# Two matmuls of one pair change places in the first entry of each group

## The chip, the cores and the metric

The kernel runs on one core of one Trainium2 chip. The metric is the device time of one execution in microseconds; lower is better. The engines are named as the profile names them: PE is TensorE's matmuls and PEld its weight loads, DVE is VectorE, ACT ScalarE, POOL GpSimd, SP SyncE.

## The reference, cut to what matters

One hybrid decoder block on 256 tokens of width 2048, all in float32:

```
x = layer_norm(ALPHA*x + 0.5*swiglu(x, ffn1 gate, up, down))     # D_FF 5632
mix = hybrid_mixer(x)        # x @ w_in, then attention heads and a gated linear recurrence, then @ w_out
x = layer_norm(ALPHA*x + mix)
x = layer_norm(ALPHA*x + 0.5*swiglu(x, ffn2 gate, up, down))
x = x + sigmoid(x @ w_ple_gate) * (p @ w_ple_proj)
```

`swiglu(x, g, u, d)` is `(silu(x @ g) * (x @ u)) @ d`. Nearly all arithmetic is matrix products of 256 tokens with weights that are read once from memory.

## The kernel before, in words

**Precision by parts.** TensorE multiplies in a reduced float32 format (fp32r). Each operand is therefore held as two: hi, the value cast to the format, and lo, the rest. A product takes hi*hi, hi*lo and lo*hi. For weights ScalarE makes hi (line 104) and VectorE lo (line 110).

**Entries.** The weights come in a planned order as entries of 256 rows x 512 columns, two halves (k = 0, 1) of 128 rows side by side. `load` starts an entry's DMA on SP's queue, `prepare_hi` and `prepare_lo` split it, `take` hands it to the matmuls, `done` gives its slot back. There are 7 slots for split entries and 10 buffers for raw ones. Both halves of an entry are split by one instruction each, but for the very first entry, which is split half by half. The order of the instructions on every engine is the order in which the program writes them.

**Groups.** Two kinds of matmul exist. `group_b` and the down products keep the activations stationary and stream 512 weight columns (`mm_moving_w`, three matmuls of 512 columns each). `group_a` keeps the weights stationary: a group computes 512 output columns as four blocks (b = 0 to 3) of 128, one PSUM bank each, over 8 entries (j = 0 to 7). For each entry `tokens_a` runs over the blocks and, inside, over the two halves. Per block and half stands a pair, `mm_stationary_w`: first a matmul with weights hi that streams the tokens' hi and lo, 2 x 256 = 512 columns, into the whole bank; then one with weights lo that streams the tokens' hi alone, 256 columns, into the bank's first half. The two half banks are added at the end by `evac_a` (ScalarE copies one, VectorE adds the other). An entry has 8 pairs, a group 64.

**Where `group_a` is used.** In each of the two feed-forward parts 11 chunks have a gate group and an up group. From the fifth group on, after every second entry (in the last chunk every entry), `product` runs part of a down projection on activations that are ready: 12 matmuls of 512 columns, put together in a scheme of seven products for four blocks. The first gate group of the second part is a boundary group: it goes over its 8 entries twice, with 128 tokens each, so that the normalisation before it can end meanwhile. In the mixer `channels` calls `group_a` six times (three for the recurrence's input, three for its gate). After each entry `tick` lets waiting work go a step: pieces of the recurrence and of attention, some of which put plain float32 matmuls and transposes on TensorE.

**Start flags.** The first matmul of a bank in a group (entry 0, half 0) clears the bank; all others add to it.

The change touches `mm_stationary_w`, `tokens_a`, `group_a` and `channels`.

Of the kernel before, what the change touches and what calls it, by code (L numbers as in the profile page):

```python
# [15 lines left out]
KB = D // P  # L16
# [24 lines left out]
class Block:  # L41
# [220 lines left out]
    def mm(self, out, lhsT, rhs, start, stop):  # L262
        self.nc.tensor.matmul(out, lhsT=lhsT, rhs=rhs, start=start, stop=stop, skip_group_check=True)  # L263

    def mm_stationary_w(self, bank, b, hi, lo, k, kb, tok, start, stop):
        bv = bank.rearrange("p (s t) -> p s t", s=2)
        c = slice(b * P, (b + 1) * P)
        self.mm(bv[:, :, tok], hi[:, k, c], self.xT[:, kb, :, tok], start, False)
        self.mm(bv[:, 0, tok], lo[:, k, c], self.xT[:, kb, 0, tok], False, stop)

    def mm_moving_w(self, bank, act, hi, lo, start, stop):
        ah, al = act
# [5 lines left out]
        ts = slice(t * P, (t + 1) * P)  # L278
        return self.xT[:, kb, 0, ts], self.xT[:, kb, 1, ts]

    def tokens_a(self, e, j, banks, tok, first, on_block=None):
        for b in range(4):
            for k in range(2):
                kb = 2 * j + k
                self.mm_stationary_w(banks[b], b, e["hi"], e["lo"], k, kb, tok, kb == 0 and first, kb == KB - 1)
            if on_block and j == 7:
                on_block(b, banks[b])

# [2 lines left out]
            kb = 2 * j + k  # L291
            self.mm_moving_w(bank[:, cols], self.x_act(kb, t), e["hi"][:, k, cols], e["lo"][:, k, cols], kb == 0, kb == KB - 1)

    def group_a(self, on_block, boundary=False, step=2):
        banks = [self.bank() for _ in range(4)]
        if not boundary:
            for j in range(8):
                e = self.take()
                self.tokens_a(e, j, banks, slice(0, 256), True, on_block)
                self.done(e)  # L300
                self.tick()
                if j % step == step - 1:
                    self.product()
            return
        es = []
        self.limit = self.taken + 8
        for j in range(8):
            es.append(self.take())
            self.tokens_a(es[j], j, banks, slice(0, P), True)
            if j == 1:  # L310
                self.advance_lo(self.ready)
            if j in HOOKS:
                self.ln_transpose(1, HOOKS.index(j))
        self.limit = len(self.plan)
        self.res_q.append(self.ln_residual())
        for j in range(8):
            self.tokens_a(es[j], j, banks, slice(P, 256), False, on_block)
            self.done(es[j])
            self.tick()
# [447 lines left out]
    def channels(self):  # L767
        got = []

        def on_block(b, bank):  # L770
            if b == 0:
                got.append(self.wide())
            self.evac_a(bank, got[0][:, b, :])

        self.group_a(on_block)
        return got[0]

    def mixer(self):
# [156 lines left out]
```

## Time and profile before

| | |
|---|---|
| median of three runs | 1920.38 us (1919.65 to 1920.59) |
| profiled execution | 1922.0 us, its span 1919.9 us |
| mean granted TensorE clock | 0.996 |
| busy: PE, PEld, DVE, ACT, POOL | 98%, 84%, 79%, 57%, 13% |
| read from memory | 413.38 MB, 216 GB/s over the span |
| matmuls with stationary weights, hi and lo | 3216 and 3216 |

The span is the time from the first to the last instruction of the profiled execution. Busy times are unions of recorded instructions; a matmul is recorded until its modelled end, and the next one starts before that, so the distance from one start to the next says what a matmul takes of TensorE's time. The chain that ended last is followed back from the last instruction, at each step to what released it.

### The profile page before, as it was taken

The numbers are of one execution on the slowest core, as the hardware profiler recorded it, in microseconds if no ns is written. First come the engines' busy times: TensorE is split into PE (matmuls) and PEld (weight loads), VectorE is DVE, ScalarE is ACT, GpSimd is POOL, SyncE is SP. The second block draws the span as 40 slices with busy tenths as digits, with TensorE's granted clock in tenths as the row PEclk, the third lists the DMA queues.
The fourth block names the chain that finished last, engine by engine and source line by source line (L and its number), as shares of the span: only waits on it lengthen the run. The fifth ranks groups of instructions, "written<-read, shape, count | busy, mean of one in ns | idle before, by whom it ended". The sixth has DMA issues, their size and how long they took to land.

```text
span 1919.9 us, 26885 instructions
## 1 busy us (share of the span) xinstructions
PE 1878.9 (98%) x10004; PEld 1614.0 (84%) x10004; DVE 1522.9 (79%) x1889; ACT 1090.7 (57%) x1440; POOL 242.4 (13%) x173
## 2 busy tenths in 40 slices
PE   8999999999999999999999999999999999999899
PEld 7888888888888777887888898888888888887787
DVE  6698887887888879577676966888879888888774
ACT  6565555555655556566655454655556555556552
POOL 0010000000010116001010250000000100011160
PEclk9999999999999999999999999999999999999999
DMA  9678688788786876655455656787887868878572
GB/s 355 218 192 265 209 254 234 207 262 244 221 253 190 232 239 211 195 178 163 143 184 178 208 181 182 241 221 216 255 253 201 260 207 253 246 207 252 179 231 76
DMA packets 216770, 417.23 MB, mean 217 GB/s; under 512 B 13232, under 2 KB 15936, under 8 KB 216640
## 3 DMA queue, kind: packets, MB, share of 16 engines
q1 hardware_dynamic: 193856, 370.42, 58.1%
q0 software_dynamic: 22784, 45.10, 13.8%
q8 instruction: 78, 1.28, 0.3%
q14 instruction: 52, 0.43, 0.1%
HBM read 413.38 MB, written 2.10 MB: 216 GB/s over the span
## 4 chain that ended last, share of the span: by engine, by line
PE 87%; DVE 7%; issue 2%; ACT 2%; DMA 1%; POOL 1%; SPq 0%; ACTq 0%; DVEq 0%; POOLq 0%
PE mm L263 86%; DVE lo L110 3%; DVE raw L82 1%; DVE w L370 1%; ACT hi L104 1%; DMA raw<-in_w_in_dram 0%; DMA raw<-in_ffn_w_gate_dram 0%; PE mm L505 0%; DVE w L556 0%; ACT w L64 0%; POOL w L110 0%; DVE w L65 0%; DMA raw<-in_ffn_w_down_dram 0%; DVE acc L495 0%; DVE acc L428 0%
## 5 line engine op out<-in xcount | busy, mean ns | idle before, releaser
L104 ACT CAST hi<-raw 128x1024 fp32r<-128x1024 f32 (+1 forms) x786 | 809.6, 1049 | 545.3 <-PE mm L263 470.6
L263 PE MATMUL mm<-xT,hi 128*128 128x512 f32 (+1 forms) x3216 | 1104.8, 390 | 6.2 <-DVE xT L65 5.2
L110 DVE TENSOR_TENSOR lo<-raw,hi 128x1024 fp32r<-128x1024 f32 (+1 forms) x786 | 950.3, 1250 | 100.1 <-ACT hi L104 90.4
L263 PE MATMUL mm<-xT,lo 128*128 128x256 f32 (+1 forms) x3216 | 888.7, 276 | 0.0
L263 PEld LDWEIGHTS mm<-xT,hi 128*128 128x128 f32 x3216 | 605.2, 188 | 132.2 <-ACT hi L104 6.5
L263 PEld LDWEIGHTS mm<-xT,lo 128*128 128x128 f32 x3216 | 606.6, 189 | 6.2 <-DVE lo L110 0.7
L263 PE MATMUL mm<-hi,w 128*128 128x512 f32 x1464 | 483.2, 394 | 13.3 <-DVE acc L428 11.0
L263 PEld LDWEIGHTS mm<-hi,w 128*128 128x128 f32 x1464 | 276.5, 189 | 76.2 <-ACT hi L104 13.7
L263 PE MATMUL mm<-lo,w 128*128 128x512 f32 x732 | 288.0, 394 | 0.0
L85 POOL DMA_DIRECT2D raw<-in_ffn_w_down_dram x80 | 96.0, 1218 | 1116.4 <-DVE raw L82 546.8
L263 PE MATMUL mm<-hi,xT 128*128 128x512 f32 (+1 forms) x544 | 168.8, 386 | 0.0
L428 DVE TENSOR_TENSOR acc<-acc,mm 128x512 f32<-128x512 f32 x124 | 84.9, 684 | 100.8 <-PE mm L263 100.8
L263 PEld LDWEIGHTS mm<-lo,w 128*128 128x128 f32 x732 | 138.5, 189 | 23.4
L263 PEld LDWEIGHTS mm<-hi,xT 128*128 128x128 f32 x544 | 101.3, 189 | 19.3
L263 PE MATMUL mm<-lo,xT 128*128 128x512 f32 (+1 forms) x272 | 104.0, 382 | 3.6 <-DVE lo L110 3.6
L370 DVE TENSOR_TENSOR w<-mm,w 128x256 f32<-128x256 f32 x200 | 83.6, 419 | 28.1 <-ACT w L369 27.6
L82 DVE TENSOR_TENSOR raw<-raw,raw 128x1024 f32<-128x1024 f32 x80 | 97.8, 1222 | 1.4
L369 ACT COPY w<-mm 128x256 f32<-128x256 f32 x200 | 72.6, 365 | 25.9 <-PE mm L263 22.3
L541 ACT ACTIVATE w<-w 128x256 f32<-128x256 f32 x88 | 36.8, 418 | 67.3 <-DVE w L370 67.3
L64 ACT CAST w<-qk 128x512 fp32r<-128x512 f32 (+1 forms) x42 | 25.5, 609 | 83.6 <-DVE qk L455 40.4
L542 DVE TENSOR_TENSOR w<-w,w 128x256 f32<-128x256 f32 x88 | 38.0, 432 | 43.4 <-ACT w L541 43.4
L508 ACT ACTIVATE qk<-mm,par 128x128 f32<-128x128 f32 x96 | 36.1, 456 | 54.3 <-PE mm L505 54.1
(136 smaller groups left out, 872.6 us busy)
## 6 DMA issues: line engine op xcount, KB each, us to landing
raw<-in_ffn_w_up_dram SPq DMA_DIRECT2D x176, 512.0 KB, 5.0
raw<-in_ffn_w_down_dram SPq DMA_DIRECT2D x176, 512.0 KB, 5.3
raw<-in_ffn_w_gate_dram SPq DMA_DIRECT2D x175, 512.0 KB, 5.5
raw<-in_w_in_dram SPq DMA_DIRECT2D x88, 512.0 KB, 4.5
raw<-in_ffn_w_down_dram POOLq DMA_DIRECT2D x80, 512.0 KB, 7.4
raw<-in_w_out_dram SPq DMA_DIRECT2D x32, 512.0 KB, 4.6
raw<-in_w_ple_gate_dram SPq DMA_DIRECT2D x32, 512.0 KB, 6.1
w<-in_ln_g_dram SPq DMA_DIRECT2D x12, 256.0 KB, 6.3
```

Source lines behind the costliest of these rows:

```text
L64: self.nc.scalar.copy(hi, src)
L82: self.nc.vector.tensor_tensor(a, a, b, op=ALU.add)
L85: self.nc.gpsimd.dma_start(a, src, accum_op=ALU.add)
L104: self.nc.scalar.copy(e["hi"][:, k, :], e["raw"][:, k, :])
L110: eng.tensor_tensor(e["lo"][:, k, :], e["raw"][:, k, :], e["hi"][:, k, :].bitcast(F32), op=ALU.subtract)
L263: self.nc.tensor.matmul(out, lhsT=lhsT, rhs=rhs, start=start, stop=stop, skip_group_check=True)
L369: self.nc.scalar.copy(c, bank[:, 256:])
L370: self.nc.vector.tensor_tensor(dst, bank[:, :256], c, op=ALU.add)
L428: self.nc.vector.tensor_tensor(a, a, bank, op=op)
L508: nc.scalar.activation(z[:, q, :], bank[:, q * P:(q + 1) * P], AF.Identity, bias=self.par[:, p0 + 16 + kb:p0 + 17 + kb], scale=self.par[:, ...
L541: nc.scalar.activation(s, g, AF.Sigmoid)
L542: nc.vector.tensor_tensor(g, g, s, op=ALU.mult)
```

## The change

In the pair of block 0, half 1, the matmul with weights lo is issued before the one with weights hi. In the feed-forward parts this is done in the first entry of each group (j = 0), in the mixer's `channels` groups in all eight entries. The number of instructions, their operands and the data moved stay the same; the two flags follow the place in the pair.

```
-    def mm_stationary_w(self, bank, b, hi, lo, k, kb, tok, start, stop):
+    def mm_stationary_w(self, bank, b, hi, lo, k, kb, tok, start, stop, low_first=False):
         bv = bank.rearrange("p (s t) -> p s t", s=2)
         c = slice(b * P, (b + 1) * P)
-        self.mm(bv[:, :, tok], hi[:, k, c], self.xT[:, kb, :, tok], start, False)
-        self.mm(bv[:, 0, tok], lo[:, k, c], self.xT[:, kb, 0, tok], False, stop)
+        high = bv[:, :, tok], hi[:, k, c], self.xT[:, kb, :, tok]
+        low = bv[:, 0, tok], lo[:, k, c], self.xT[:, kb, 0, tok]
+        one, two = (low, high) if low_first else (high, low)
+        self.mm(*one, start, False)
+        self.mm(*two, False, stop)
...
-    def tokens_a(self, e, j, banks, tok, first, on_block=None):
+    def tokens_a(self, e, j, banks, tok, first, on_block=None, turn=False):
...
-                self.mm_stationary_w(banks[b], b, e["hi"], e["lo"], k, kb, tok, kb == 0 and first, kb == KB - 1)
+                self.mm_stationary_w(banks[b], b, e["hi"], e["lo"], k, kb, tok, kb == 0 and first, kb == KB - 1,
+                                     b == 0 and k == 1 and (turn or j == 0))
...
-    def group_a(self, on_block, boundary=False, step=2):
+    def group_a(self, on_block, boundary=False, step=2, turn=False):
...
-                self.tokens_a(e, j, banks, slice(0, 256), True, on_block)
+                self.tokens_a(e, j, banks, slice(0, 256), True, on_block, turn)
...
-        self.group_a(on_block)
+        self.group_a(on_block, turn=True)
```

The last two lines are those of `channels`.

## Rows read from the trace of the kernel before

**Rows 1.** Page: slices (PEclk in tenths) and the chain, by engine.

```profile
PEclk9999999999999999999999999999999999999999
...
PE 87%; DVE 7%; issue 2%; ACT 2%; DMA 1%; POOL 1%; SPq 0%; ACTq 0%; DVEq 0%; POOLq 0%
```

**Rows 2.** Timeline of PE at 982 us; columns: start us, duration us, instruction, tiles.

```profile
982.00 0.39 PE L263 MATMUL mm<-xT,hi 128*128 128x512 f32 x1
982.22 0.28 PE L263 MATMUL mm<-xT,lo 128*128 128x256 f32 x1
982.34 0.39 PE L263 MATMUL mm<-xT,hi 128*128 128x512 f32 x1
```

**Rows 3.** Timeline of PE at 1134 us.

```profile
1134.00 0.40 PE L263 MATMUL mm<-xT,hi 128*128 128x512 f32 x1
1134.23 0.28 PE L263 MATMUL mm<-xT,lo 128*128 128x256 f32 x1
1134.35 0.39 PE L263 MATMUL mm<-xT,hi 128*128 128x512 f32 x1
```

**Rows 4.** Groups by line and shape, 12.84 to 104.4 us; busy us, mean ns, idle.

```profile
L263 PE MATMUL mm<-xT,hi 128*128 128x512 f32 x263 | 92.4, 395 | 0.0
L263 PE MATMUL mm<-xT,lo 128*128 128x256 f32 x262 | 73.7, 281 | 0.0
```

**Rows 5.** Groups by line and shape, 180 to 480 us.

```profile
L263 PE MATMUL mm<-xT,hi 128*128 128x512 f32 x616 | 211.6, 389 | 0.0
L263 PE MATMUL mm<-xT,lo 128*128 128x256 f32 x615 | 169.9, 276 | 0.0
```

**Rows 6.** Windows: length, busy us (x count) by engine, PEclk, DMA share, GB/s.

```profile
795.10:821.60 26.50, 26.50 (x151) 23.29 (x150) 10.86 (x12) 18.85 (x30) 2.40 (x1) 1.00 0.50 152
934.50:958.60 24.10, 22.65 (x137) 19.97 (x136) 13.64 (x24) 17.64 (x29) 3.09 (x2) 1.00 0.45 128
1124.40:1199.70 75.30, 75.30 (x428) 66.13 (x427) 49.05 (x64) 36.48 (x52) 7.05 (x6) 1.00 0.62 184
```

**Rows 7.** Timeline of PE at 1199.7 us, behind a product.

```profile
1199.75 0.40 PE L263 MATMUL mm<-xT,hi 128*128 128x512 f32 x1
1199.98 0.28 PE L263 MATMUL mm<-xT,lo 128*128 128x256 f32 x1
1200.10 0.39 PE L263 MATMUL mm<-xT,hi 128*128 128x512 f32 x1
```

**Rows 8.** Timeline of PE at 794 us, plain fp32 matmuls of the recurrence.

```profile
793.95 1.03 PE L263 MATMUL mm<-w,w 128*128 128x256 f32 x4
```

**Rows 9.** Timeline of PE at 1205.2 us, the start of a product.

```profile
1205.20 0.40 PE L263 MATMUL mm<-hi,w 128*128 128x512 f32 x1
1205.43 0.40 PE L263 MATMUL mm<-lo,w 128*128 128x512 f32 x1
1205.67 0.62 PE L263 MATMUL mm<-hi,w 128*128 128x512 f32 x2
```

**Rows 10.** Timeline of PE at 1912 us, 256-column matmuls of the last group.

```profile
1911.98 0.40 PE L263 MATMUL mm<-hi,xT 128*128 128x256 f32 x2
1912.22 0.28 PE L263 MATMUL mm<-lo,xT 128*128 128x256 f32 x1
```

**Rows 11.** Chain of waits, a piece of 55 to 124 us: start us, us, what.

```profile
75.22 0.28 ACT w L369
```

**Rows 12.** Timeline of PE at 122.85 us; in brackets idle time before it, releaser.

```profile
122.85 0.47 PE L263 MATMUL mm<-hi,w 128*128 128x512 f32 x1 [1.38 <-DVE acc L426]
```

**Rows 13.** Chain of waits, its longest piece: start us, us, what.

```profile
1109.60 582.02 PE mm L263 x3215
```

**Rows 14.** Timeline of PE at 8 us, the first entry.

```profile
8.01 0.58 PE L263 MATMUL mm<-xT,lo 128*128 128x256 f32 x1
8.38 0.63 PE L263 MATMUL mm<-xT,hi 128*128 128x512 f32 x1
...
8.81 0.41 PE L263 MATMUL mm<-xT,lo 128*128 128x256 f32 x1
```

## The prediction

> **What bounds the kernel now.** I read the page first: the slices and the chain that ended last, then single stretches of TensorE in order of time, then the groups of matmuls by shape. The page says that TensorE sets the time: it holds 87% of the chain that ended last, and its granted clock is at 9 tenths or more in every slice [rows 1]. So a change in the order of matmuls is worth what it does to the spacing of matmul starts, and no view of waits would show that. The reader should therefore go to the timeline of TensorE and take differences of starts. Call the 512-column matmul of a pair (weights hi) H and the 256-column one (weights lo) L. Both belong to one pair on one weight block.
>
> The stream H L H L runs at two paces. At 982 us an H is followed by its L after 0.22 to 0.23 us and the next H comes 0.34 us after the last one [rows 2]. At 1134 us the same instructions, with the same shapes and no wait, need 0.35 us per pair: 0.23 and 0.12 [rows 3]. The rows by shape say it finer: in the stretch from 12.84 to 104.4 us one H takes 395 ns and one L 281 ns in the mean [rows 4], in the stretch from 180 to 480 us 389 and 276 ns [rows 5]. That is 6 + 5 = 11 ns a pair by durations, 10 ns by starts; I use 10. The granted clock is 1.00, the 2.4 GHz level, in the slow stretches too [rows 6], so this isn't the clock. I call the two paces fast and slow; each holds for dozens of pairs without a break.
>
> Where are the slow stretches? From 12.84 to 104.4 us (263 pairs), 795.1 to 821.6 (72), 934.5 to 958.6 (54) and 1124.4 to 1199.7 (208) [rows 4, 6]: half the matmuls of a window are its pairs, once 8 and 29 of the recurrence and attention and 12 of a product are taken off. Together some 590 pairs of 10 ns, 5.9 us: no change of pace alone can win more. What stands ahead of a stretch tells which pace it has. After a product, twelve 512-column matmuls in a row, the stream takes one long pair (H to L 0.23, L to H 0.12) and is fast from there [rows 7]. After plain fp32 matmuls of the recurrence it is slow [rows 6, 8], and so it is from the start of the program and from the end of the boundary group. The slow stretches are thus the groups with no product between their entries. A run of 512-column matmuls puts the stream right; nothing inside H L H L does.
>
> **The change part by part.** It adds and removes no instruction, no byte and no wait. In one pair of an entry it turns H L H L H into H L L H H: one start of L after L, and one of H after H, which the stream of pairs never has. In the feed-forward parts this happens once a group (11 chunks x 2 groups x 2 parts = 44, and once more in the second half of the boundary group), in the mixer in all 8 entries of 6 groups: 93 turns.
>
> Cost of a turn in a fast stream. The nearest rows for H after H behind an L are the first matmuls of a product: 0.23 and 0.24 us [rows 9], some 0.015 us more than twice the 0.227 that an H has of a fast pair's 0.340 by its two thirds of the columns. The pair behind it is then the long one that follows a product, whose L takes 0.12 in place of 0.11: 5 ns. L after L is nearest to the 256-column matmuls at the end, 0.24 us for two starts [rows 10], 120 ns against 113: 7 ns at most, by the L's third of the 0.340. So a turn costs 0 (if the order is free) to 27 ns; I take 20, which the product's rows carry.
>
> Gain of a turn in a slow stream. This the trace does not show. From below it is 0 or the cost above. From above the turn's H H acts as the end of a product does, and the stream is fast behind it. I take the second, because the pairs behind a turn have the neighbours of the pairs behind a product: an H that follows a 512-column matmul and is followed by an L [rows 7]. Then:
> - First feed-forward part. The first group's turn falls in the first entry, at 8 us, before the stream has a pace. The groups without products have 4 x 64 + 16 = 272 pairs up to 104.4 us, 263 of them in the slow stretch, so 9 lie before 12.84 us, the first group has 55 in it, and the second starts at 12.84 + 55 x 0.35 = 32 us. From there to 104.4 us are 72 us or 206 pairs, 2.1 us. But not all of it arrives: from 75.22 us on the chain runs over the evictions and VectorE [rows 11], and TensorE waits 1.38 us for it at 122.85 us [rows 12]. So only 32 to 75 us counts, 43 / 0.35 = 123 pairs, 1.2 us; the other 0.9 us lengthens that wait.
> - Second feed-forward part: 206 of 208 pairs, 2.1 us. TensorE alone holds the chain for 582 us from 1109.60 us [rows 13], so it arrives.
> - Mixer: 72 + 54 pairs, of which 6 in 8 lie behind a turn: 94 pairs, 0.9 us; a part of the second stretch waits for attention anyway, so 0.75.
>
> Sum of the gains 4.05 us. Costs: turns that fall in a fast stream are 44 + 1 - 11 (five groups of the first part, four of the second, two halves of the boundary group) = 34 in the feed-forward parts and some 32 of the mixer's 48 (the slow stretches hold 126 / 8 = 16 entries): 66 x 20 ns = 1.3 us. The 27 other turns cost the same 20 ns less what they win: 0.4 us. The boundary group's two turns, of half-width matmuls, have no row near them and are counted with these.
>
> Start of the program. In the first entry lo of the second weight half comes late: L starts at 8.01 us, and the next H at 8.38 [rows 14], while H of that half had run in front, hidden behind the wait for lo. Now that H comes after L: up to the 0.43 us that one takes there (8.81 less 8.38 us) is exposed, less the 0.16 us by which the H at 8.38 came later than an L of half that length would let it: 0.3 us.
>
> Everything else that is moved lies under cover. Both weight halves of an entry come from one instruction in all other entries, so the earlier L waits for nothing new: the L before it waited for the same subtraction. In the last entry of a mixer group, the first bank's high half is ready one L (0.11 us) later, so one eviction of the first block starts later; three blocks of matmuls, some 2 us, follow before TensorE could miss the bank. No DMA and no queue is passed.
>
> Net: 1.3 + 0.4 + 0.3 - 4.05 = -2.05 us. The profiled execution was 1922.0 us with a span of 1919.9; it would be 1920.0 and 1917.9. The median of the runs is 1920.38, 1.6 below the profiled one; I forecast 1920.38 - 2.05 = 1918.3 us.
>
> One rule speaks against the whole argument. The Trainium skill, "TensorE: Matmul & The Clock Gate", section "Back-to-back issue gap", gives an isolated gap of columns / 2.4 + 2.5 ns at the full clock: 216 ns for H and 109 for L, whatever stands beside them. By that an H L pair is 325 ns in any order, and the change is worth nothing. The rows have 340 and 350 for the same pair at the same clock, so the formula alone does not carry here; but a pace that depends on no order would be the second rival below.
>
> **The rivals.**
> (a) The turn puts a fast stream into the slow pace. For it: each fast stream was entered from a run of 512-column matmuls, never from less, and other breaks (fp32 matmuls, the end of the boundary group, the cold start) all left the stream slow [rows 6, 8]. Against it: H behind H is what ends a product. Place and price: 30 feed-forward groups with a product every second entry lose 6 + 8 pairs each, the four groups of last chunks 6, together 444 pairs, 4.4 us; the mixer's 32 fast entries 7 pairs each, 2.2 us; the 0.3 of the start and the 66 turns, 1.3. Sum +8.2: 1928.6 us. It decides once the pair behind the turn falls into the slow pace in more than about a third of the fast groups.
> (b) The order is free or the pace stays as it was: slow stretches stay slow, fast ones fast. Cost 0.3 to 0.3 + 93 x 20 ns = 2.2 us: 1920.7 to 1922.6.
> (c) The turn wins all and costs nothing, and the first part's 0.9 us arrives too: -4.9 + 0.3 = -4.6, 1915.8 us. Against it: the wait of 1.38 us at 122.85 belongs to VectorE's chain.
>
> **How the numbers follow.** A kernel of this spread tells no change from one within 0.2%, 3.8 us: 1916.5 to 1924.2. The forecast case, 1916 to 1920 us, has 0.45; (a) 0.17; (b) 0.25; (c) 0.13. Faster by over 0.2%: all of (c) and a third of the forecast case, 0.28. Slower: (a), 0.17, and a little of (b) with a part of (a) in it, 0.02, together 0.19. Within: the rest, 0.53. For 8 in 10 the range goes from 1915.3 (below (c)) to 1924.5 (above (b), and a partial (a)); all of (a) at its full price is what it leaves out.
>
> **What would show it.** If the forecast is right, H takes 389 and L 276 ns in the mean in the windows of rows 4 and behind 1127 us, pairs come every 0.34 us there from the second group on, the wait at 122.85 us is longer by up to 1 us, and the products of the middle of each part come at the same distance as before or some 0.02 us more for one in four. If (a) holds, the pairs between a group's first entry and its next product show 395 and 281 ns. If (b), rows 3 and 4 look as they do now. I am wrong on the price of a turn if H L L H H between fast pairs is not some 20 ns longer than H L H L H. A change in waits of TensorE anywhere but at the start and at 122.85 us would show a mechanism that I have not seen.

## The result, and the profile after

The changed kernel takes 1932.23 us in the median of four runs (1931.97 to 1933.19), the kernel before beside it 1920.09 us (1919.65 to 1920.59). The medians are 12.1 us apart. The ratio is 1.0054, its 95% interval 1.0036 to 1.0072: slower by some half a per cent, where 0.1% faster was forecast. The profiled execution is 1932.03 us with a span of 1929.9 us, 10.0 us more than the span before; the accounts below are of these 10.0 us.

The page hides it, as it hid the two paces before: TensorE is busy for 98% of the span and every slice of the granted clock shows 9 tenths, as in [rows 1]. The chain of waits shows where the time went. Its long pieces are runs of matmuls in which TensorE waits for nothing, so their lengths can be compared directly. Columns: start us, length us, what, number of instructions. First the kernel before, where the fourth long piece is the one in [rows 13]:

```profile
122.85 478.31 PE mm L263 x2583
741.52 107.61 PE mm L263 x568
955.76 125.08 PE mm L263 x620
...
1838.66 76.86 PE mm L263 x384
```

and the changed kernel:

```profile
123.06 481.14 PE mm L263 x2583
744.60 108.50 PE mm L263 x568
959.70 126.04 PE mm L263 x620
1114.47 584.52 PE mm L263 x3215
...
1848.68 76.86 PE mm L263 x384
```

The same number of matmuls, no wait, and each piece is longer: by 2.83 us (rest of the first feed-forward part), 0.89 and 0.96 (mixer) and 2.50 (second part; 584.52 against the 582.02 of [rows 13]), 7.18 us together. The starts give the rest. At 122.85 us the kernel is 0.21 us late, between 604 and 744 us nothing is added (0.04), nor on either side of the third piece (0.03 less on each), from 1699 to 1848 us another 2.65.

What lengthens the pieces is seen behind a product. The timeline of TensorE in the changed kernel, at the first group whose first entry follows one; "x2" puts two starts into one row:

```profile
134.06 0.40 PE L263 MATMUL mm<-xT,hi 128*128 128x512 f32 x1
134.30 0.40 PE L263 MATMUL mm<-xT,lo 128*128 128x256 f32 x2
134.53 0.63 PE L263 MATMUL mm<-xT,hi 128*128 128x512 f32 x2
135.00 0.28 PE L263 MATMUL mm<-xT,lo 128*128 128x256 f32 x1
135.12 0.40 PE L263 MATMUL mm<-xT,hi 128*128 128x512 f32 x1
```

In [rows 7] the stream is fast one pair after the product. Here three pairs, the turn among them, take 135.12 - 134.06 = 1.06 us, 0.02 more than the same three pairs of the kernel before, 134.90 - 133.86 = 1.04:

```profile
133.86 0.40 PE L263 MATMUL mm<-xT,hi 128*128 128x512 f32 x1
...
134.90 0.39 PE L263 MATMUL mm<-xT,hi 128*128 128x512 f32 x1
```

The pairs behind them come every 0.35 us up to the next product, which ends at 142.45 us. Groups by shape of the changed kernel over 180 to 480 us show the mixture (columns as in [rows 5]): 391 and 277 ns where [rows 5] have 389 and 276.

```profile
L263 PE MATMUL mm<-xT,hi 128*128 128x512 f32 x610 | 210.3, 391 | 0.0
L263 PE MATMUL mm<-xT,lo 128*128 128x256 f32 x611 | 168.0, 277 | 0.0
```

In the groups without products each turn gives a pace to a whole group. Groups by shape of the changed kernel where [rows 4] were slow throughout: behind the turn of the first group (14.1 to 31.2 us), of the second (33 to 54 us) and of the fourth (78.2 to 98.5 us):

```profile
L263 PE MATMUL mm<-xT,hi 128*128 128x512 f32 x52 | 17.7, 389 | 0.0
L263 PE MATMUL mm<-xT,lo 128*128 128x256 f32 x51 | 14.1, 276 | 0.0
...
L263 PE MATMUL mm<-xT,hi 128*128 128x512 f32 x61 | 21.6, 395 | 0.0
L263 PE MATMUL mm<-xT,lo 128*128 128x256 f32 x60 | 16.8, 281 | 0.0
...
L263 PE MATMUL mm<-xT,hi 128*128 128x512 f32 x60 | 20.4, 389 | 0.0
L263 PE MATMUL mm<-xT,lo 128*128 128x256 f32 x61 | 16.8, 276 | 0.0
```

The third group has 395 and 281 ns again. By the starts of their H the pairs of the four groups come every 340.0, 353.3, 350.0 and 340.0 ns in the mean: the slow pace is two paces.

The last 2.65 us are the granted clock. Windows of 5 us (columns as in [rows 6]: length, busy us of PE, PEld, DVE, ACT, POOL, granted clock, DMA share, GB/s), the changed kernel behind a wait of 3.1 us of TensorE for the last normalisation:

```profile
1810.00:1815.00 5.00, 1.86 (x8) 1.46 (x7) 2.21 (x5) 0.40 (x2) 2.75 (x2) 0.74 0.60 183
1815.00:1820.00 5.00, 5.00 (x16) 3.98 (x16) 4.17 (x7) 4.97 (x11) 0.00 (x0) 0.58 0.07 27
```

and the kernel before, at the same work behind the same wait:

```profile
1805.00:1810.00 5.00, 3.87 (x21) 3.33 (x22) 4.21 (x8) 3.17 (x7) 0.41 (x1) 1.00 0.45 145
1810.00:1815.00 5.00, 5.00 (x27) 4.15 (x26) 4.93 (x7) 4.97 (x11) 0.00 (x0) 1.00 0.32 96
```

In the slow window 16 matmuls fit into 5 us where 27 fit at full clock. This stretch at the 1.2 GHz level is not bound to the changed order: in a second profiled execution (below) the four long pieces are 481.14, 108.52, 126.05 and 584.52 us, the same to 0.02 us, but the last piece of 384 matmuls starts at 1843.75 us, 4.93 us earlier than here. Of these, 0.66 us are there at 122 us; 1.70 arise between 604 and 742 us and 2.54 between 1697 and 1844 us, behind the long waits. So the pieces repeat and the clock behind the long waits does not.

### The profile page after: what moved, and what is told of

It reads as the page before. It is cut to its first block, busy times and chain, and to the rows that moved or that the text cites. A ratio compares the mean times of both kernels' runs of the same rounds, so it can differ in the third digit from the quotient of the medians.

```text
span 1929.9 us, 26885 instructions
## 1 busy us (share of the span) xinstructions
PE 1888.3 (98%) x10004; PEld 1618.5 (84%) x10004; DVE 1521.8 (79%) x1889; ACT 1091.5 (57%) x1440; POOL 241.3 (13%) x173
## 4 chain that ended last, share of the span: by engine, by line
PE 89%; DVE 6%; issue 2%; ACT 2%; POOL 1%; DMA 0%; SPq 0%; ACTq 0%; DVEq 0%; POOLq 0%
PE mm L263 88%; DVE lo L110 3%; DVE raw L82 1%; DVE w L374 1%; PE mm L509 0%; ACT hi L104 0%; DVE w L560 0%; DMA raw<-in_ffn_w_gate_dram 0%; ACT w L64 0%; POOL w L110 0%; DVE w L65 0%; DVE acc L499 0%; DVE acc L432 0%; ACT w L545 0%; DVE w L546 0%
## 5 line engine op out<-in xcount | busy, mean ns | idle before, releaser
L263 PE MATMUL mm<-xT,lo 128*128 128x256 f32 (+1 forms) x3216 | 876.0, 277 | 1.6 <-DVE lo L110 1.6
L263 PEld LDWEIGHTS mm<-xT,hi 128*128 128x128 f32 x3216 | 599.0, 188 | 126.1 <-ACT hi L104 5.1
```

## The experiments

In what follows "first part" and "second part" are the feed-forward parts, "pieces" the four long pieces of the chain above (478.31, 107.61, 125.08 and 582.02 us before). Times are medians; a ratio is to the kernel before, run on the same chip, as recorded with its interval (it is not the quotient of the medians). The kernel before had a median of 1920.86 us beside experiments 1 to 4, 1921.02 beside 5 to 7, 1922.87 beside 8 and 9 and 1921.77 beside 10 to 12. Pairs are timed by the starts of their H.

**The changed kernel a second time,** with no edit.

> The changed kernel once more, beside the kernels below. Theory A (pace alone) counts 3.0 us in the first feed-forward part, 1.9 in the mixer and 2.5 in the second, 7.4 in all: 1927.5 us for a run whose half-clock stretches are those of the kernel before. Theory C (the rest of the 12.1 us is where the half-clock stretches fall, which changes from run to run): single runs between 1926 and 1933 us, the slower ones at a lower mean granted clock. If the 12.1 us belong to the change itself, all runs stand near 1932.

Measured: 1930.98 us (1927.10 to 1932.97) against 1921.02, ratio 1.0049 (1.0033 to 1.0066). The profiled execution is its shortest, 1927.10 us, with the pieces of the first one.

**1. The turns in the feed-forward parts alone.** Against the changed kernel:

```
-                                     b == 0 and k == 1 and (turn or j == 0))
+                                     b == 0 and k == 1 and turn and j == 0)
...  (turn=True in the groups of swiglu, none in channels)
```

> Only the feed-forward groups keep their turn (first entry, block 0, half 1); the mixer's groups issue as before. Theory A (a turn in a fast stream leaves the slow pace behind it until the next run of 512-column matmuls; a turn in a slow stream sometimes leads out of it): 187 ns a group where products follow, in all +5.5 us, 1925.6 us. Theory B (what a turn costs is its own place, and each of the 93 turns costs the same, 12.1 us / 93 = 130 ns): 45 turns, +5.9 us. Theory C (most of the +12.1 is half-clock windows that fall otherwise): no more than +3 from the pace, the rest where the granted clock falls.

Measured: 1927.17 us, ratio 1.0040 (1.0029 to 1.0052). The pieces are 481.18, 107.61, 125.06 and 584.52: the feed-forward parts as in the changed kernel, the mixer as before.

**2. The mixer's turns alone.**

```
-                                     b == 0 and k == 1 and (turn or j == 0))
+                                     b == 0 and k == 1 and turn)
```

> Only the mixer's six groups keep their turns, 48 of the 93. Theory A: about +1.9 us, 1922.0 us, since two of three entries run slow behind a turn and one fast, where before some 126 of the 384 pairs were slow. Theory B: 48 x 130 ns = +6.3 us, 1926.4 us. Theory C: +2 to +5 us, all of it in stretches at the half clock.

Measured: 1924.20 us, ratio 1.0016 (1.0006 to 1.0026). Pieces 478.29, 108.53, 126.11 and 582.02. The two halves of the change add up, piece by piece, within 0.1 us. In the profiled execution the granted clock is 0.55 from 1810 to 1815 us on top, behind the same wait, with no turn near it.

**3. The feed-forward turn moved to just ahead of a product.**

```
-                                     b == 0 and k == 1 and (turn or j == 0))
+                                     b == 2 and k == 1 and turn and j == 1)
```

> The turn of the feed-forward groups moves from the first entry, block 0, to the second entry, block 2: one pair of blocks ahead of the product that puts the stream right; none in the mixer. Theory A: only the turn's own 40 ns and two slow pairs are left for a group with products, about 60 ns, +2.2 us for 36 groups, less or more by what the turns do to the nine groups without products; 1922 us. Theory B: as with the turn in its old place, +5.9 us, 1926.0 us.

Measured: 1924.01 us, ratio 1.0010 (0.9998 to 1.0022). Pieces 479.00, 107.61, 125.07 and 582.30. As many turns as in experiment 1, but the pieces of the two parts lengthen by 0.69 and 0.28 us in place of 2.87 and 2.50. So the turn itself is cheap (0.69 us over 15 groups, with one slow pair behind each); what costs is the number of pairs between it and the next product.

**4. No turns, but eight L and then eight H in two entries.** Against the kernel before:

```
+    def tokens_apart(self, e, j, banks, tok):
+        for part in ("lo", "hi"):
+            for b in range(4):
+                for k in range(2):
...  (the L or the H of the pair)
```

used in the fourth entry of the first gate group and the second entry of the second part's first up group.

> No turns. In two entries (fourth of the first feed-forward group, second of the group behind the boundary group) the eight lo matmuls are issued first and the eight hi matmuls behind them, so that a run of eight 512-column matmuls stands ahead of the slow stretches. Theory A with a run of 512-column matmuls as the cure: pairs come every 340 ns from there to the next break, 2.0 us less in the second part and 1.2 to 2.6 us less in the first, less 0.1 us for each of the two entries: 1916 to 1917 us. If the length of the run is not what cures, or the slow pace comes from the place in the program: 1920 us, 350 ns a pair as before.

Measured: 1920.16 us, ratio 1.0000 (0.9987 to 1.0013); pieces 478.30, 107.61, 125.07, 582.08. The timeline of this kernel at the first of the two entries:

```profile
18.06 0.40 PE L263 MATMUL mm<-xT,hi 128*128 128x512 f32 x1
18.30 1.24 PE L263 MATMUL mm<-xT,lo 128*128 128x256 f32 x9
19.37 2.26 PE L263 MATMUL mm<-xT,hi 128*128 128x512 f32 x9
21.47 0.28 PE L263 MATMUL mm<-xT,lo 128*128 128x256 f32 x1
21.59 0.40 PE L263 MATMUL mm<-xT,hi 128*128 128x512 f32 x1
21.82 0.28 PE L263 MATMUL mm<-xT,lo 128*128 128x256 f32 x1
21.94 0.39 PE L263 MATMUL mm<-xT,hi 128*128 128x512 f32 x1
```

Nine starts of H take 21.47 - 19.37 = 2.10 us, 233 ns each, and the next pair takes 0.35 as the pairs before did. A run of 512-column matmuls with weights hi leaves a slow stream slow. What the prediction took from [rows 7] as the cure was therefore not the length of the run; what else in a product does it, no run here tells.

**5. H H L H L ... H L L in the first entry of each feed-forward group:** the H stand one place ahead, the last two L come together. Against the kernel before, in `tokens_late_lo`:

```
+                self.mm(bv[:, :, tok], e["hi"][:, k, c], self.xT[:, kb, :, tok], kb == 0, False)
+                if late:
+                    self.mm(*late.pop(), False, False)
+                late.append((bv[:, 0, tok], e["lo"][:, k, c], self.xT[:, kb, 0, tok]))
+        self.mm(*late.pop(), False, False)
```

> In the first entry of each full feed-forward group the lo matmul of each pair comes one pair late (H H L H L ... H L L): H behind H stands at the start of the entry, L behind L at its end, and the stream between them alternates as ever. If H behind H throws a fast stream into the slow pace, the first entry's pairs take 350 ns and the group is 150 ns longer than before. If L behind L does it, the first entry stays at 340 ns, the second runs at 350, and a group is 80 to 100 ns longer. If only the two together do it, both entries stay at 340.

Measured in a single execution: 1923.47 us; pieces 480.76, 107.61, 125.10, 583.90. The L L at the end of the entry in the second part's first up group, in this kernel's timeline:

```profile
1127.34 0.40 PE L263 MATMUL mm<-xT,hi 128*128 128x512 f32 x1
1127.57 0.28 PE L263 MATMUL mm<-xT,lo 128*128 128x256 f32 x1
1127.69 0.40 PE L263 MATMUL mm<-xT,hi 128*128 128x512 f32 x1
1127.93 0.40 PE L263 MATMUL mm<-xT,lo 128*128 128x256 f32 x2
1128.16 0.39 PE L263 MATMUL mm<-xT,hi 128*128 128x512 f32 x1
1128.39 0.28 PE L263 MATMUL mm<-xT,lo 128*128 128x256 f32 x1
1128.50 0.39 PE L263 MATMUL mm<-xT,hi 128*128 128x512 f32 x1
```

0.35 us per pair before the L L, 0.34 behind it, and the next such entry at 1149 us made it 0.35 again until 1200 us. A slow stream can thus be made fast by L L. The experiment also parts the two breaks of a turn, as it was meant to: the H H of the entry at 1147 us stands in a fast stream, and by starts the pairs behind it are 340 ns again after one of 355; the L L at its end, at 1149.71 us, leaves 350. The entry at 31 us shows the same. So it was the L L that ended a fast stream, two times out of two; H H alone did not, though it took slow streams from 350 to 353 ns.

**6. The place of the weight tiles.** Against the kernel before; LINE shifts the weights hi of `group_a` inside their tiles, and every tile of weights hi is 4 x LINE elements longer, so with LINE = 0 the tiles lie closer together too:

```
-LINE = 16
+LINE = 0
```

> The kernel before with the tiles of stationary hi weights at offset 0 in place of 16 elements (64 bytes): the same instructions in the same order. If the two paces come from how weight loads and streams meet in memory, the paces themselves change: by the steady rows of unshifted operands (512 columns each 227 ns, 256 columns each 120 ns) one pair would take 347 ns in all stretches, some +13 us. If the pace depends on the order of lengths alone, the stretches stay at 340 and 350 as before, 1920 us.

Measured in a single execution: 1950.81 us. The order is that of before, and neither pace is: over 300 to 500 us the groups by shape of this kernel are

```profile
L263 PE MATMUL mm<-xT,hi 128*128 128x512 f32 x405 | 143.9, 398 | 0.0
L263 PE MATMUL mm<-xT,lo 128*128 128x256 f32 x404 | 113.4, 281 | 0.0
```

where [rows 5] have 389 and 276; by starts pairs come at 353.3 ns, in one stretch from 1142 to 1212 us (205 pairs) at 346.7, and no stretch is at 340. So the fast pace belongs to how the operands of the pair lie in memory as well as to the order. In the same kernel the fourth piece is 593.20 us in place of 582.02.

**7. The changed kernel with one turn in either part,** at the start of the first part's first up group and, in the second part's, in block 2 of the second entry:

```
-                                     b == 0 and k == 1 and (turn or j == 0))
+                                     (b, k, j) == turn)
...
+            self.group_a(on_up, step=step, turn=((2, 1, 1) if boundary else (0, 1, 0)) if c == 0 else None)
```

> Two turns in the whole kernel, both in slow streams: second feed-forward group of the first part (first entry, block 0) and the group behind the boundary group (second entry, block 2), the places where the earlier kernels with turns were seen to go from slow to fast. Theory A: 340 ns a pair from there to the first product; 2.0 us less in the second part, 1.2 us less in the first (the rest goes into the wait at 122.85 us): 1917 to 1918 us. If a turn costs by its own place only: 1921 us.

Measured: 1924.66 us, ratio 1.0020 (1.0010 to 1.0031); the granted clock is 0.50 from 1805 to 1810 us in the profiled execution. Pieces 478.31, 107.64, 125.08, 582.68. The first turn cured its stream, groups by shape of this kernel over 33 to 100 us:

```profile
L263 PE MATMUL mm<-xT,hi 128*128 128x512 f32 x199 | 67.7, 389 | 0.0
L263 PE MATMUL mm<-xT,lo 128*128 128x256 f32 x198 | 54.6, 276 | 0.0
```

The piece behind it starts at 121.20 us, 1.65 us earlier than before: here the gain that the forecast counted on is real, and arrives. The second turn left its stream slow, by starts at 353.3 ns in place of 350.0, and the piece is 0.66 us longer.

**8. Two cures:** the first turn of experiment 7, and the order of experiment 5 in the second part's first up group alone.

```
+                if turn == "late" and j == 0:
+                    self.tokens_late_lo(e, j, banks, slice(0, 256))
...
+            self.group_a(on_up, step=step, turn=("late" if boundary else (0, 1, 0)) if c == 0 else None)
```

> Two places alone, both in a stream that is at 350 ns a pair before. First feed-forward part: one pair L H in the first entry of the up group behind the first gate group; a single such turn there brought pairs of 340 ns from 32.65 to 101.67 us and 1.66 us that arrived. Second part: in the first entry of the up group behind the boundary group the order H H L H L ... H L L; in the kernel with this order in every group the L L there brought 340 ns from 1128 us on, until the next L L. Theory A (the pace flips with each break of the alternation and then stays till a product): some 200 pairs of 340 in place of 350 ns in either part, 1.7 us in the first and 1.8 to 2.0 us in the second, so 3.5 us at equal clock, near 1917 us; the mixer unchanged. If the stretch at half clock at about 1806 us comes up as in some other kernels, 3.4 us of it are lost and the time is near 1920. Theory B (which of the paces follows is not set by the break but by where the stream stands in time when it comes, so the same edit need not give the same pace once 1.7 us have shifted it): the second part stays at 350 ns or starts fast by itself and is turned slow; then 1.7 us at most, 1918.5 us, and the pairs from 1126 to 1198 us show 350 ns.

Measured: 1924.21 us (1917.91 to 1924.67), ratio 0.9999 (0.9987 to 1.0011). Pieces 478.32, 107.61, 125.08 and 580.04: the L L won 1.98 us of the fourth piece. The turn cured nothing this time, groups by shape over the same 33 to 100 us:

```profile
L263 PE MATMUL mm<-xT,hi 128*128 128x512 f32 x190 | 67.2, 396 | 0.0
L263 PE MATMUL mm<-xT,lo 128*128 128x256 f32 x191 | 53.7, 281 | 0.0
```

Up to there the kernels of experiments 7 and 8 are the same instructions. Ahead of the turn both have pairs of 350.0 ns in the mean (13 to 31 us); behind it one has 340.0, the other 353.3. So the order alone doesn't say which pace a break leaves. The traces do show a difference ahead of the turn. In a stream at 350 ns the distances from H to H alternate, 349 and 351 ns or 348 and 352; the last one ahead of the turn was the longer in experiment 7 (351) and the shorter here (349). What the second part won was lost in the clock, windows of this kernel:

```profile
1705.00:1710.00 5.00, 3.00 (x11) 2.21 (x10) 4.32 (x6) 3.98 (x5) 0.72 (x1) 0.80 0.55 196
1710.00:1715.00 5.00, 5.00 (x25) 4.24 (x24) 4.26 (x5) 2.10 (x2) 1.70 (x2) 0.86 0.78 120
1800.00:1805.00 5.00, 1.87 (x9) 1.32 (x8) 1.07 (x3) 0.00 (x0) 3.89 (x3) 0.85 0.41 114
1805.00:1810.00 5.00, 5.00 (x17) 4.12 (x16) 4.17 (x8) 4.22 (x8) 0.00 (x0) 0.50 0.27 96
```

**9. LINE = 8** in place of 16, the edit of experiment 6 with another number.

> The constant LINE, which sets an offset of 16 between tiles in memory in the kernel before, is 8 here; order of the matmuls as before. With LINE 0 pairs came at 346.7 or 353.3 ns in place of 340 or 350. Theory A (the two paces hang on how the streams of a pair lie to each other in memory): the paces are other than 340 and 350 again, or their places in time change, and the time moves by some us. Theory B (LINE 0 is a special case, any other offset is alike): pairs at 340 and 350 in the same stretches, and 1920 us.

Measured in a single execution: 1947.14 us, and the distances from H to H change every few pairs, most of them between 346 and 352 ns, and none is 340. The fourth piece is 591.88 us.

**10 to 12. The wait at 1803 us filled,** in the kernel before, in the changed kernel and in that of experiment 8. Twelve matmuls whose results are not used run where TensorE waits:

```
+        if fill:
+            for _ in range(12):
+                self.mm(bank, *fill, True, True)
```

ahead of the transposes of `ln_transpose(0, 0)`, in the last normalisation alone, with an operand of the down product and weights that are already there.

> The kernel before, with twelve 512-column matmuls more, whose results are not used (each writes the bank that the transposes behind it overwrite), ahead of the first transposes of the last normalisation, where TensorE waits 3.13 us for VectorE at 1803 us. 12 x 0.227 = 2.7 us of that wait are filled. Theory A (the granted clock falls to 0.5 behind that wait because TensorE idles in it): no half-clock stretch from 1803 to 1820 us in any run, the runs lie closer together, near 1919 to 1921 us, and none at 1925 to 1928. Theory B (the fall comes from elsewhere): runs spread as before, 1919 to 1928.

> The changed kernel with the same twelve unused matmuls in the same wait. Theory A (order costs 8 us by its pace, the rest is the clock behind the wait): 8 us over e12_fill, so 1927 to 1929 us, the granted clock 1.00 behind the wait. Theory B (the tail's loss belongs to the turns): 10 us or more over e12_fill, with a stretch at 0.5 in the tail in spite of the matmuls.

> The kernel e9_two_cures with the same twelve unused matmuls. Its profiled run was 3.1 us ahead of the kernel before at 1700 us, lost 1.6 us in a half-clock stretch behind the wait at 1706 us and 2.7 us in one behind the wait at 1801 us. Theory A: the second of these is gone; some 2.0 to 3.5 us under e12_fill and 1917 us or less, depending on whether the turn at 32 us gives 340 ns in the run. Theory B (tail's fall not from the idle wait): 1921 to 1924 as e9_two_cures.

Measured: kernel before with fill 1921.24 us (1918.02 to 1925.11; ratio 0.9997, 0.9988 to 1.0006), changed kernel with fill 1929.73 us (1929.34 to 1932.06; 1.0046, 1.0033 to 1.0060), two cures with fill 1919.58 us (1918.86 to 1922.49; 0.9990, 0.9981 to 0.9999). Windows of the changed kernel with fill, behind the wait:

```profile
1810.00:1815.00 5.00, 4.64 (x23) 3.62 (x22) 1.75 (x4) 0.46 (x2) 3.21 (x3) 1.00 0.49 167
1815.00:1820.00 5.00, 5.00 (x27) 4.15 (x26) 4.68 (x8) 4.96 (x10) 0.00 (x0) 1.00 0.11 43
```

The granted clock stays at 1.00 there, in the profiles of all three. Of the twelve profiles without the fill seven have a stretch at the 1.2 GHz level behind this wait, that of experiment 9 among them, which has no turn at all (granted clock 0.68 from 1830 to 1835 us). So that loss goes with the wait in which TensorE idles, not with the turns; that the fill always prevents it, three profiles don't prove.

With it gone the changed kernel stands 8.5 us over the kernel before, by the medians and by the spans (1927.6 and 1919.1 us). This is not yet the price of the order alone. Between the two profiles the pieces differ by 2.85, 0.92, 1.03 and 2.50, 7.3 us; the first piece starts 1.35 us earlier in the changed kernel (121.91 against 123.26); and 2.5 us lie between the pieces, behind the waits at 664 and 1717 us, where its granted clock fell lower (0.52 against 0.72 from 665 to 670 us; 0.77 and 0.89 from 1715 to 1725 us, where the other has 1.00 behind the same wait).

The other half of theory A failed: the runs of the kernel before spread as widely as without the fill, so that wait is not the only thing that moves them. The two cures with fill are 2.2 us under the kernel before (1921.77 us beside it), by an interval that just excludes no change and by less than the 0.2% that the prediction called none; the L L won the same 1.98 us again (fourth piece 580.04), and the turn at 32 us again left 353.3 ns, its last distance ahead being the shorter one (348).

## Why the prediction was wrong

The forecast was 1918.3 us, 2.05 us faster; the medians have 12.1 us slower. Two steps failed, a price and a gain.

**The price of a turn in a fast stream** was 20 ns, taken from rows of a product's start, which price the turn's own starts. Those came out right: the three pairs at a turn take 0.02 us more than the same pairs before. But the pace behind the turn was counted as kept, without a row for it, and it is lost. Each such turn makes the pairs up to the next product slow, 14 of them in the feed-forward groups: in the first part's long piece 15 groups became 0.16 to 0.21 us longer, most 0.19, 2.83 us in all, in place of 0.02 us each.

**The gain of a turn in a slow stream** failed with it: "From above the turn's H H acts as the end of a product does, and the stream is fast behind it. I take the second". The upper end was taken because the pairs behind a turn have the neighbours of the pairs behind a product. Neighbours don't decide it: nine H in a row leave a slow stream slow (experiment 4), one turn left the same stream fast in one kernel and slow in another (7 and 8). Of the groups without products in the second part, which were to win 2.1 us, the changed kernel won 0.37 us up to 1201 us.

I counted the turns in the nine profiles that have some, by the distances from one H start to the next ahead of the turn and behind it:

| pace ahead of the turn | pace behind it | turns |
|---|---|---|
| 340 ns | 353 ns | 92 of 92 |
| 353 ns | 350 ns | 58 of 58 |
| 350 ns, the last distance the longer of the two | 340 ns | 64 of 64 |
| 350 ns, the last distance the shorter | 353 ns | 5 of 5 |
| none yet, one pair behind a product | 350 ns | 112 of 112 |

Behind other matmuls, nearly all of them in the mixer, a turn left 340 ns 22 times, 350 ns 10 times and 353 ns 8 times. So a turn ends every fast stream, and of 127 turns in slow ones half (64) lead out; a stream at 353 ns needs two. This is why in the mixer, and in the groups without products, every third turn sets the stream fast. The table is a reading of traces: no run changed the place of a turn in the alternation and nothing else.

**Rival (a)** describes what happened, and its sum was nearly right. It put 4.4 us on 444 feed-forward pairs, and with its turns (34 x 20 ns) and 0.3 at the start 5.4 us; the pieces and the start show 2.83 + 2.50 + 0.21 = 5.5. For the mixer it had 2.8 us, measured 1.8: it left every stream slow behind a turn, and there every third turn sets it fast again. In all it said +8.2; the pieces and the start sum to 7.4. That the two kernels with fill differ by 8.5 is in part luck: 2.5 of it is clock (above). What should have raised its chance over 0.17 stood in the argument itself: "each fast stream was entered from a run of 512-column matmuls, never from less, and other breaks ... all left the stream slow". I set against it one likeness, of H behind H with a product's end, which no row tested in that form. A pace that four fifths of the pairs have (by the prediction's count 590 of 3216 are slow) and that is entered behind one kind of event alone is the state that a break can lose.

**The first part.** The forecast had a gain of 1.2 us arriving from 32 to 75 us. In the changed kernel the first and the fourth group were fast, the second and the third slow (above). The stretch up to 122.85 us ended 0.21 us late; the wait of [rows 12] is 1.43 us in place of 1.38, not up to 1 us longer, and a wait of 0.28 us stands at 105.42 us, where the kernel before has none:

```profile
105.42 0.73 PE L263 MATMUL mm<-hi,w 128*128 128x512 f32 x2 [0.28 <-DVE w L65]
...
123.06 0.47 PE L263 MATMUL mm<-hi,w 128*128 128x512 f32 x1 [1.43 <-DVE acc L430]
```

Where a turn did cure that stretch (experiment 7), 1.65 us arrived, more than the 1.2 counted: the wait for VectorE, there 0.58 us at 103.56 us, took little of it. The 0.21 us is no firm number: this piece starts at 123.06, 122.40 and 121.91 us in three profiles of the changed order, at 122.85 and 123.26 us in two of the order before.

**The second part** and the mixer were to gain 2.1 and 0.75 us; they lost 2.50 (0.37 won up to 1201 us, 2.87 lost behind it) and 1.8.

**The start** was priced at 0.3 us from [rows 14]. L waits 1.64 us for the late half now, and H comes behind it:

```profile
7.89 0.58 PE L263 MATMUL mm<-xT,lo 128*128 128x256 f32 x1 [1.64 <-DVE lo L110]
8.27 1.05 PE L263 MATMUL mm<-xT,hi 128*128 128x512 f32 x2
9.12 0.41 PE L263 MATMUL mm<-xT,lo 128*128 128x256 f32 x1
```

L comes at 9.12 where it came at 8.81: 0.31 us, as priced, but by luck. The first L came 0.12 us earlier here; from it to the L behind are 1.23 us in place of 0.80, so all of the 0.43 us was exposed, and the 0.16 us taken off it was not there to take. That no other wait of TensorE moves held for the long ones, those over 1 us are the same within 0.12 us; the short one at 105.42 us is new.

**What the prediction didn't have** is the clock behind the long waits: 2.65 us of the profiled 10.0, present in some executions and not in others, with turns and without. "So this isn't the clock" was right for the two paces and wrong as a bound for the runs.

The rule that was weighed, the Trainium skill's "TensorE: Matmul & The Clock Gate", section "Back-to-back issue gap", gives columns / 2.4 + 2.5 ns for an isolated matmul, from which 325 ns for the pair was estimated, and says that in a stream the weight loads take part in the spacing. The formula alone doesn't reach this stream: the same pair at the same granted clock took 340, 347, 350 and 353 ns.

**Open:** why the paces are these, and what sets the alternation of a stream when a turn meets it. That the order alone doesn't decide the pace behind a break is shown by experiments 7 and 8; that the place of the weights in memory counts, by 6 and 9, one execution each. Which of the streams of a pair meet, and where, no run here tells.

## What to carry to other kernels

Where the same instructions run at two paces in one trace, take the differences of starts, find out what stands ahead of each pace, and treat the shorter as something that any break of the pattern may end: count what the edit does to the stretches that have it already before what it may mend in the others. Compare long pieces of the chain without waits before medians: here they repeat to 0.1 us, while the clock moves the whole run by some microseconds. A break can be useful behind a slow start, one at a time and measured by its piece; whether it is, differed here between executions of the same instructions.

## What the runs showed of the hardware that was not expected

- One pair of a 512-column and a 256-column matmul ran at 340.0, 346.7, 350.0 and 353.3 ns at a granted clock of 1.00, each for dozens of pairs: steps of 6.7 or half of that. A turn moved the stream from 340 to 353 ns, from 353 to 350 and from 350 to 340 or 353, in 219 cases without an exception.
- The slow pace itself differs between executions: the first part's slow stretch had pairs of 350.0 ns in the kernel before and 353.3 ns in the same instructions of the kernel with fill.
- LINE = 16 in the place and length of the tiles of weights hi is worth some 30 us here (1950.81 us with 0, against 1921.02); with 8 in its place the kernel is some 24 us slower (1947.14 against 1922.87). Both are single executions.
- Twelve matmuls with no use, put into a wait of 3.1 us, left the granted clock behind it at 1.00 in three profiles of three; without them it fell to 0.5 there in seven of twelve.
